# Six PSUM banks in a convolutional FFN, a later attention with two-part fp32r sums, and one sum moved to VectorE

## The chip, the cores and the metric

The kernel runs on one core of a Trainium2 chip. The metric is the device time of one execution in microseconds (us). Five engines work side by side, each through its own queue in program order: TensorE (PE: matmul, and PEld: its weight loads), VectorE (DVE), ScalarE (ACT), GpSimd (POOL) and SyncE (SP). PE multiplies a stationary operand (lhsT) by a moving one and writes to banks of PSUM; the other engines read the banks.

## The reference, cut to what matters

A sequence of 256 tokens of width 1024 passes through two blocks: a conformer convolution with a convolutional FFN, then two layers of FFN, mixer, FFN. The first layer's mixer is a recurrence, the second's is stick-breaking attention with 12 heads, together with an attention over 256 memory tokens. Three parts are touched here:

```python
def conv_ffn(h, w_up, dw_w, dw_b, w_down):
    u = causal_dwconv(h @ w_up, dw_w) + dw_b          # 3 taps
    gt, v = jnp.split(u, 2, axis=-1)
    return (jax.nn.silu(gt) * v) @ w_down

# stick-breaking attention, one block of 128 queries
z = einsum('bhtd,bhsd->bhts', q, k) * scale
log_keep = where(before, -softplus(z), 0.0)
later = cumsum(log_keep, axis=3, reverse=True) - log_keep
att = where(before, exp(log_sigmoid(z) + later), 0.0)
out = einsum('bhts,bhsd->bhtd', att, v)
```

The third is the mean and variance over the width after each mixer's output projection.

## The kernel before

Every large product is made of three fp32r products: activations and weights are each split into a high part and a low part. A weight unit (128 x 1024) is brought by DMA, cast to its high part by ACT (line 226, `whi`) and subtracted to its low part by DVE (line 235, `wlo`); `Stream.take` hands out units and issues the splits of units that come four later. The order on every engine is that of the program; there is no scheduler behind it.

**Convolutional FFN** (`ffn` with `conv`). For each of 22 hidden tiles j, PE makes two products into one PSUM bank (lines 372, 377 and 378, 48 matmuls), and `conv_gate` reads that bank: two ACT passes (line 885), four DVE passes (line 889), then silu (ACT, 894), a product (DVE, 895), a cast to `hx` high (ACT, 896) and a subtraction to `hx` low (DVE, 898). The bank is free again after line 889. Tiles 0 and 1 use banks acc2 and acc3, all later ones two `gu` banks in turn. Then the down projection (lines 372 and 384) runs for each of 8 outputs over all 22 `hx` tiles.

**Stick-breaking mixer** (`StickBreaking`). `weave` writes out one order of several tasks by a plan: each task yields its estimated PE time, DVE time and an extra delay; the plan keeps a clock for PE (`now`) and one for DVE, takes the first task in order of priority that is due, and where none is due it emits filler matmuls (`idle`, line 1455, 256 columns, one for each 0.11 us of the plan's gap). The main task makes the projections; attention has the highest priority; once the main task has ended, products of the output projection join. For each of 6 pairs of heads attention goes through these steps, shifted so that pair p's scores come before pair p-1's sums: `scores` (PE, then |z| and exp on ACT, lines 2298 and 2299), `log_keep` (Ln on ACT, line 2305, a DVE pass, line 2306, and a mask on POOL, line 2308), `attend` (three fp32 matmuls per head that add the running sums to the bank `z`, lines 2316, 2317 and 2319, a DVE pass and an exp on ACT), `values` (PE, lines 2332 and 2334, then a copy on ACT and a split, lines 625 and 626). The products of the output projection wait in the plan until five pairs have gone through `attend`. The constants for the mask and the sums (`sbc`, 320 KB) are brought by a DMA on ACT's queue at the start of the mixer.

**Output projection's end** (`gemm_tail`, at the end of three square products: line 1348 sums, line 1358 merge). The squares and values of tiles 0 to 3 are summed on POOL, those of tiles 4 and 6 on DVE, then the two sums are merged on DVE, tile 7 is taken out of its bank, and PE reduces the sums over partitions (line 1383).

Of the kernel before, what the change touches and what calls it, by code (L numbers as in the profile page):

```python
# [250 lines left out]
class Builder:  # L251
# [217 lines left out]
    def gemm_tail(self, acc, xs, st, on_tiles):  # L469


        def tile(w, b, o, i):
            c = slice((2 * i + o) * P, (2 * i + o) * P + P)
            self.mm3(acc[b][:, o, :], w[0][:, c], w[1][:, c], xs[i], False,
                     i == self.NT - 1)

        ws = [self.stream.take(False) for _ in range(2)]
        n = self.NT - 1
        for i0, i1 in ((0, n), (n, n + 1)):
            for b in range(2):  # L480
                for i in range(i0, i1):
                    for o in range(2):
                        tile(ws[b], b, o, i)
                if b == 0:
                    self.stream.split_hi()
        self.stream.split_hi()
        self.stream.split_lo()
        for b in range(2):
            on_tiles(2 * b, 2 * b + 2, acc[b])
            st.square(2 * b, 2 * b + 2)  # L490
            st.sum(2 * b, 2 * b + 2, "pool")
            if b == 0:
                self.stream.split_lo()
        ws = [self.stream.take(False) for _ in range(2)]
        self.stream.split_hi()
        for k in (4, 6, 5, 7):
            b, o = divmod(k, 2)
            for i in range(self.NT):
                tile(ws[b - 2], b, o, i)
            on_tiles(k, k + 1, acc[b][:, o:o + 1, :])  # L500
            st.square(k, k + 1)
            if k == 4:
                self.stream.split_lo()
            elif k == 5:
                st.sum(4, 5, "dve")
                st.sum(6, 7, "dve")
                st.sum(5, 6, None)
                st.merge()
        st.sum(7, 8, None)
        self.stream.split_lo()  # L510
# [270 lines left out]
    def ffn(self, conv, st, on_tile, li=None):  # L781


        self.mark("ffn")
        with self.pool("ffn") as self.fp:
            hs = [self.fp.tile([P, 2, T], F32R, name=f"hx{j}") for j in range(NF)]
            gates = []

            def gate(j, banks):
                make = self.conv_gate if conv else self.wide_gate  # L790
                gates.append(make(banks, j, hs[j][:, 0, :], hs[j][:, 1, :]))
                next(gates[-1])

            def advance():
                for g in list(gates):
                    if next(g, 0) == 0:
                        gates.remove(g)

            def banks(j):
                if conv:  # L800
                    return [self.acc_tile(2 + j) if j < 2 else self.gu_tile()]
                return [self.gu_tile() for _ in range(2)] if j % 3 == 0 else [
                    self.acc_tile(2 * (j % 3) - 2 + o) for o in range(2)]

            n = 0
            if self.pre is not None:
                for n in range(2):
                    gates.append(self.pre_gate(self.pre[2 * n:2 * n + 2], hs[n][:, 0, :], hs[n][:, 1, :]))
                    next(gates[-1])
                n = 2  # L810
                self.pre = None
            first = [banks(n), banks(n + 1)]
            (self.gemm_outs if conv else self.gemm_wides)(first[0] + first[1], self.xx)
            for j, bk in enumerate(first):
                gate(n + j, bk)
                advance()
                advance()
            for j in range(n + 2, NF):
                bk = banks(j)
                for o in range(2):  # L820
                    if conv:
                        self.gemm_out(bk[0][:, o, :], self.xx)
                    else:
                        self.gemm_wide(bk[o], self.xx)
                    advance()
                gate(j, bk)
            self.mark("down")
            self.preload(AF.Sqrt)
            if li is not None:
                self.raw_gains(li)  # L830
            i = 0
            for o in range(KD):
                acc = self.acc_tile(o % 4)
                for j in range(NF):
                    if i % 8 == 0:
                        wh, wl = self.stream.take()
                    c = slice(i % 8 * P, i % 8 * P + P)
                    self.mm_wide(acc, wh[:, c], wl[:, c], hs[j], j == 0, j == NF - 1)
                    i += 1
                    if o == 0 and j in (4, 8):  # L840
                        advance()
                on_tile(o, acc)
                st.square(o, o + 1)
                if li is not None:
                    self.raw_operand(o, li)
                st.sum(o, o + 1, "pool")
                if o < KD - 1:
                    self.pump(3.0)
# [1306 lines left out]
class StickBreaking(Mixer):  # L2155
# [25 lines left out]
    def project(self):  # L2181
        nc, b, mp = self.nc, self.b, self.mp
        sbc = mp.tile([P, 640], F32, name="sbc")
        nc.scalar.dma_start(out=sbc, in_=b.dr["consts_sb"])
        b.exp_and_log()
        self.sbk = {n: sbc[:, COFF[n][0]:sum(COFF[n])] for n, _ in CONSTS_SB}
        self.negones = mp.tile([P, P], F32, name="negones")
        nc.gpsimd.memset(self.negones, -1.0)
        ys = b.ys.rearrange("p k a t -> p (k a) t")
        self.V = ys[:, 0:6].rearrange("p (a f) t -> p a (f t)", a=2)  # L2190
        self.os = ys[:, 6:12]
        self.mq = ys[:, 14:16]
        self.qk, self.n_val = {}, 0
        pre, b.pre = b.pre, None
        for i in range(2):
            nc.scalar.copy(out=self.mq[:, i, :], in_=pre[2 + i])
        self.qk[0] = pre[:2]
        self.add(self.attention(), 1)
        for tl in range(2):
            self.add(self.mem_attention(tl, ys[:, 12 + tl]), SB_MEM)  # L2200
        early = [b.gu_tile() for _ in range(2)]
        yield from b.gemm_outs_parts(early, b.xx)
        for n in range(2):
            self.queries(n + 1, [early[n][:, i, :] for i in range(2)])
        self.mem_go = True
        for kind, i in SB_ORDER[2:]:
            if kind == "p":
                yield from self.pair(i)
                continue
            gu = b.gu_tile()  # L2210
            for u in range(2):
                list(b.gemm_tok(gu, b.xx, u))
                if u:
                    nc.scalar.copy(out=self.V[:, :, i * T:i * T + T], in_=gu)
                    self.n_val += 1
                yield 2.6, 1.1, 0.0
# [40 lines left out]

    def attention(self):

        yield 0.0, 0.0, 7.0  # L2260
        self.n_att = 0
        prev = None
        for p in range(NP + 1):
            cur = None
            if p < NP:
                wait = p not in self.qk
                while p not in self.qk:
                    yield
                if wait:
                    yield 0.0, 0.0, 1.0  # L2270
                cur = [self.scores(h, *self.qk[p]) for h in range(2)]
                yield 1.3, 0.9, 0.0
            if prev:
                for z, e in prev:
                    self.attend(z, e)
                self.n_att = p
                yield 1.7, 0.9, 0.0
            if cur:
                for z, e in cur:
                    self.log_keep(z, e)  # L2280
                yield 0.0, 0.9, 0.0
            if prev:
                while self.n_val <= (p - 1) // 2:
                    yield
                yield from self.values(p - 1, prev)
            prev = cur
# [21 lines left out]
        nc.gpsimd.tensor_tensor(out=d, in0=d,  # L2308
                                in1=self.sbk["tri"].unsqueeze(1).to_broadcast([P, 2, P]), op=ALU.mult)

    def attend(self, z, e):

        nc = self.nc
        mm = nc.tensor.matmul
        nt = self.sbk["negtri"]
        mm(z[:, 0:256], lhsT=nt, rhs=e[:, 0:256], start=False, stop=True, skip_group_check=True)  # L2316
        mm(z[:, 128:256], lhsT=self.negones, rhs=e[:, 256:384], start=False, stop=True,
           skip_group_check=True)
        mm(z[:, 256:384], lhsT=nt, rhs=e[:, 256:384], start=False, stop=True, skip_group_check=True)
        nc.vector.scalar_tensor_tensor(out=e, in0=z, scalar=0.0, in1=self.sbk["bias"], op0=ALU.min,  # L2320
                                       op1=ALU.add)
        nc.scalar.activation(out=e, in_=e, func=AF.Exp)
# [38 lines left out]
```

## Time and profile before

| | |
|---|---|
| median of 3 runs | 1480.18 us (1478.29 to 1483.04) |
| profiled execution, its own time | 1478.92 us |
| its span in the profile | 1477.1 us |
| busy: PE, DVE, ACT, POOL | 1412.8, 1074.2, 853.8, 120.2 us |
| mean granted TensorE clock | 0.976 of full |

The span runs from the first to the last instruction; the execution's own time is 1.8 us longer. Busy times are sums over an engine's instructions. Full clock is 2.4 GHz, the lower of the two levels is 1.2 GHz.

### The profile page before, as it was taken

The page shows a single profiled execution, that of the slowest core. Times are in us where ns is not written, and L with a number is a line of the kernel's source. Part 1 is how long each engine was busy: PE and PEld are TensorE (multiplying, and loading weights), DVE is VectorE, ACT ScalarE, POOL GpSimd, SP SyncE. Part 2 cuts the span into 40 slices and gives each one's busy share as a digit, 9 for nine tenths or more (in the row PEclk, how much of TensorE's full clock was granted, in tenths as well). Part 3 has the DMA queues.
Part 4 walks back from the last instruction along what each step waited for, and adds up shares of the span by engine and source line. Part 5 has one row for each costly group of instructions (what it writes and reads, how often), then busy time and mean ns, then how long its engine had stood idle before and what let it go on. Part 6 is the DMA issues. An engine that isn't in the chain of part 4 may idle for free. (4 is left out here: it accounts for less than half of the span.)

```text
span 1477.1 us, 26067 instructions
## 1 busy us (share of the span) xinstructions
PE 1412.8 (96%) x10664; PEld 1268.2 (86%) x10664; DVE 1074.2 (73%) x1698; ACT 853.8 (58%) x1509; POOL 120.2 (8%) x113
## 2 busy tenths in 40 slices
PE   8888899999999999998999999999999999999997
PEld 7868799998788888898798888888888888888886
DVE  8897788885777667897578776687766755787754
ACT  7686566685656535751346555466554666566542
POOL 1210100001000010040010000110001111100011
PEclk9998899999999999998999999999999999999998
DMA  9775445566355554330034555436545332265540
GB/s 377 295 232 191 178 145 198 200 222 218 124 201 191 200 187 149 109 121 3 2 114 171 200 179 192 184 133 226 195 176 199 126 141 86 95 225 194 198 174 29
DMA packets 39145, 250.38 MB, mean 170 GB/s; under 512 B 4337, under 2 KB 4849, under 8 KB 12274
## 3 DMA queue, kind: packets, MB, share of 16 engines
q1 hardware_dynamic: 38594, 247.60, 46.4%
q8 instruction: 84, 1.38, 0.4%
q10 hardware_dynamic: 432, 1.11, 0.2%
q14 instruction: 35, 0.29, 0.1%
HBM read 247.65 MB, written 1.05 MB: 168 GB/s over the span
## 5 line engine op out<-in xcount | busy, mean ns | idle before, releaser
L235 DVE TENSOR_TENSOR wlo<-wraw,whi 128x1024 fp32r<-128x1024 f32 x416 | 514.4, 1250 | 33.8 <-ACT whi L226 33.2
L226 ACT CAST whi<-wraw 128x1024 fp32r<-128x1024 f32 x416 | 426.4, 1045 | 23.8 <-PE acc L378 6.4
L384 PE MATMUL acc<-hx,whi 128*128 128x512 f32 x880 | 310.8, 398 | 0.0
L384 PE MATMUL acc<-xx,whi 128*128 128x512 f32 x816 | 284.1, 390 | 0.0
L372 PE MATMUL gu<-xx,wlo 128*128 128x256 f32 x1008 | 278.3, 281 | 2.8 <-ACT xx L625 1.7
L372 PE MATMUL acc<-xx,wlo 128*128 128x256 f32 x1008 | 279.4, 282 | 0.0
L372 PE MATMUL acc<-hx,wlo 128*128 128x256 f32 x880 | 247.5, 281 | 0.0
L384 PEld LDWEIGHTS acc<-hx,whi 128*128 128x128 f32 x880 | 165.4, 188 | 40.6
L372 PEld LDWEIGHTS gu<-xx,wlo 128*128 128x128 f32 x1008 | 188.6, 188 | 7.0 <-ACT xx L625 2.9
L372 PEld LDWEIGHTS acc<-xx,wlo 128*128 128x128 f32 x1008 | 189.6, 190 | 0.8
L384 PEld LDWEIGHTS acc<-xx,whi 128*128 128x128 f32 x816 | 153.2, 188 | 32.1
L372 PEld LDWEIGHTS acc<-hx,wlo 128*128 128x128 f32 x880 | 166.1, 189 | 0.0
L384 PE MATMUL gu<-xx,whi 128*128 128x512 f32 x432 | 150.9, 390 | 0.0
L377 PE MATMUL gu<-xx,whi 128*128 128x256 f32 x512 | 148.0, 289 | 2.3 <-ACT u L894 2.3
L378 PE MATMUL gu<-xx,whi 128*128 128x256 f32 x512 | 143.1, 279 | 0.0
L1331 ACT ACTIVATE ys<-ys 128x256 f32<-128x256 f32 (+1 forms) x66 | 28.6, 436 | 152.2 <-DVE ys L1249 135.2
L377 PEld LDWEIGHTS gu<-xx,whi 128*128 128x128 f32 x512 | 96.2, 188 | 9.2 <-issue 6.4
L378 PEld LDWEIGHTS gu<-xx,whi 128*128 128x128 f32 x512 | 96.3, 188 | 0.7 <-issue 0.7
L384 PEld LDWEIGHTS gu<-xx,whi 128*128 128x128 f32 x432 | 81.1, 188 | 17.0
L1348 POOL TENSOR_TENSOR nsum<-ys 128x512 f32<-128x512 f32 (+1 forms) x9 | 12.5, 1386 | 900.0 <-PE acc L384 451.8
L858 ACT COPY lows<-acc 128x256 f32<-128x256 f32 x55 | 20.6, 374 | 97.8 <-PE acc L384 97.7
L1247 DVE SCALAR_TENSOR_TENSOR ys<-xr,acc 128x256 f32<-128x256 f32 x32 | 13.5, 422 | 74.8 <-PE acc L384 74.8
(412 smaller groups left out, 2342.0 us busy)
## 6 DMA issues: line engine op xcount, KB each, us to landing
wraw<-in_w SPq DMA_DIRECT2D x208, 1024.0 KB, 4.8
mraw<-in_mod SPq DMA_DIRECT2D x48, 512.0 KB, 5.8
xr<-in_x SPq DMA_DIRECT2D x2, 512.0 KB, 4.3
m<-in_mem SPq DMA_DIRECT2D x1, 1024.0 KB, 8.2
out<-xr SPq DMA_DIRECT2D x3, 256.0 KB, 2.2
cst<-in_consts SPq DMA_DIRECT2D x1, 546.0 KB
lora<-in_lora ACTq DMA_DIRECT2D x1, 384.0 KB, 3.2
lora_g<-in_lora ACTq DMA_DIRECT2D x1, 384.0 KB, 3.8
```

The costliest lines, as they stand in the source:

```text
L226: b.nc.scalar.copy(out=hi, in_=raw)
L235: b.nc.vector.tensor_tensor(out=lo, in0=raw, in1=hi.bitcast(F32), op=ALU.subtract)
L372: self.nc.tensor.matmul(out, lhsT=wl, rhs=x[:, 0, :], start=start, stop=False, skip_group_check=True)
L377: mm(out, lhsT=wh, rhs=x[:, 0, :], start=start, stop=False, skip_group_check=True)
L378: mm(out, lhsT=wh, rhs=x[:, 1, :], start=False, stop=False, skip_group_check=True)
L384: self.nc.tensor.matmul(bank, lhsT=wh, rhs=x, start=False, stop=stop, skip_group_check=True)
L858: nc.scalar.copy(out=lows[:, 1, :], in_=banks[1][:, 1, :])
L1247: self.nc.vector.scalar_tensor_tensor(out=y, in0=self.xr[:, k, :], scalar=2 * ALPHA, in1=ps[:, 1, :], op0=ALU.mult, op1=ALU.add)
L1331: b.nc.scalar.activation(out=b.ys[:, k0:k1, 1, :], in_=y, func=AF.Square)
L1348: e.tensor_tensor(out=out[:, q:2, :], in0=prev[:, q:2, :], in1=t[:, q:2, :], op=ALU.add)
```

## The change

Two commits together. The convolutional FFN takes six banks in turn (acc2, acc3, gu, gu, acc0, acc1). In the stick-breaking mixer, attention may begin only once the early query products are copied out (`self.early`) instead of 7 us into the plan; the softplus values are split by ACT and DVE into two fp32r parts (`e_parts`, a step of its own with 1.1 us of DVE in the plan), and each running sum is made of two fp32r matmuls instead of one fp32; the constant operands are made in fp32r by two ACT passes that read `sbc`, where POOL set one of them before. In `gemm_tail` the sum over tile 3 goes from POOL to DVE.

```diff
@@ gemm_tail
             st.square(2 * b, 2 * b + 2)
-            st.sum(2 * b, 2 * b + 2, "pool")
+            st.sum(2 * b, 2 * b + 2 - b, "pool")
             if b == 0:
                 self.stream.split_lo()
+            else:
+                st.sum(3, 4, "dve")
@@ ffn, banks
                 if conv:
-                    return [self.acc_tile(2 + j) if j < 2 else self.gu_tile()]
+                    i = (2, 3, None, None, 0, 1)[j % 6]
+                    return [self.gu_tile() if i is None else self.acc_tile(i)]
@@ StickBreaking.project
-        self.negones = mp.tile([P, P], F32, name="negones")
-        nc.gpsimd.memset(self.negones, -1.0)
+        self.negs = mp.tile([P, 2, P], F32R, name="negs")
+        nc.scalar.copy(out=self.negs[:, 0, :], in_=self.sbk["negtri"])
+        nc.scalar.activation(out=self.negs[:, 1, :], in_=self.sbk["negtri"], func=AF.Copy, scale=0.0,
+                             bias=-1.0)
...
-        self.qk, self.n_val = {}, 0
+        self.qk, self.n_val, self.early = {}, 0, False
...
-        self.mem_go = True
+        self.mem_go = self.early = True
@@ attention
-        yield 0.0, 0.0, 7.0
         self.n_att = 0
+        while not self.early:
+            yield
...
             if prev:
-                for z, e in prev:
-                    self.attend(z, e)
+                parts = [self.e_parts(e) for _, e in prev]
+                yield 0.0, 1.1, 0.0
+                for (z, e), x in zip(prev, parts):
+                    self.attend(z, e, x)
                 self.n_att = p
-                yield 1.7, 0.9, 0.0
+                yield 0.9, 0.9, 0.0
@@ attend
+    def e_parts(self, e):
+        x = self.mp.tile([P, 2, 384], F32R, name="ep", bufs=2)
+        self.b.split_act(x[:, 0, :], x[:, 1, :], e)
+        return x
...
-        nt = self.sbk["negtri"]
-        mm(z[:, 0:256], lhsT=nt, rhs=e[:, 0:256], start=False, stop=True, skip_group_check=True)
-        mm(z[:, 128:256], lhsT=self.negones, rhs=e[:, 256:384], start=False, stop=True,
-           skip_group_check=True)
-        mm(z[:, 256:384], lhsT=nt, rhs=e[:, 256:384], start=False, stop=True, skip_group_check=True)
+        for i, (w, out, c) in enumerate(((0, z[:, 0:256], slice(0, 256)), (1, z[:, 128:256], slice(256, 384)),
+                                         (0, z[:, 256:384], slice(256, 384)))):
+            for q in range(2):
+                mm(out, lhsT=self.negs[:, w, :], rhs=x[:, q, c], start=False, stop=True,
+                   skip_group_check=True)
```

The order of instructions moves with it. On ACT, at the start of the mixer, these rows stand behind the DMA of the constants before (`pre` are the first pair's products, `q` and `k` the early queries' copies, lines 2231 and 2232):

```order
L2184 DMA sbc<-in_consts_sb 128x640
L342 ACT_TABLE_LOAD
L2196 COPY ys<-pre_8478 128x256
L2196 COPY ys<-pre_8479 128x256
L226 CAST whi<-wraw 128x1024 x2
L2298 ACTIVATE e<-z 128x384
L2299 ACTIVATE e<-e 128x384
L2298 ACTIVATE e<-z 128x384
L2299 ACTIVATE e<-e 128x384
L2231 ACTIVATE q<-gu 128x256
L2232 COPY k<-gu 128x256
```

And these of the change (its lines 2192 and 2193 make the fp32r constants, 2237 and 2238 are the copies):

```order
L2187 DMA sbc<-in_consts_sb 128x640
L342 ACT_TABLE_LOAD
L2192 CAST negs<-sbc 128x128
L2193 ACTIVATE negs<-sbc 128x128
L2202 COPY ys<-pre_8478 128x256
L2202 COPY ys<-pre_8479 128x256
L226 CAST whi<-wraw 128x1024 x2
L2237 ACTIVATE q<-gu 128x256
L2238 COPY k<-gu 128x256
```

The first pair's four passes moved from ahead of the copies to behind them, and two passes that read the DMA's data came in ahead of everything.

On PE, behind the main task's last product, these rows stand before, from the first filler (line 1455) to the fifth pair's sums, which the output projection's products follow:

```order
L1455 MATMUL gu<-whi 128x256 x3
L2294 MATMUL z<-q,k 128x256
L2295 MATMUL z<-q,k 128x128
L2294 MATMUL z<-q,k 128x256
L2295 MATMUL z<-q,k 128x128
L1455 MATMUL gu<-whi 128x256 x2
L1535 MATMUL gu<-mpt_13032,memv 64x256
L1535 MATMUL gu<-mpt_13033,memv 64x256
L2316 MATMUL z<-e,sbc 128x256
L2317 MATMUL z<-e,negones 128x128
```

And of the change, at the same place, the last one and a half of three such rounds (fillers are its line 1458, sums 2332, values 2346 and 2348, scores 2303 and 2304):

```order
L1458 MATMUL gu<-whi 128x256 x22
L2332 MATMUL z<-ep,negs 128x256 x2
L2332 MATMUL z<-ep,negs 128x128 x4
L2332 MATMUL z<-ep,negs 128x256 x2
L2332 MATMUL z<-ep,negs 128x128 x4
L1458 MATMUL gu<-whi 128x256 x20
L2346 MATMUL gu<-e,ys 64x256
L2348 MATMUL gu<-e,ys 64x128
L2346 MATMUL gu<-e,ys 64x256
L2348 MATMUL gu<-e,ys 64x128
L1458 MATMUL gu<-whi 128x256 x11
L2303 MATMUL z<-q,k 128x256
```

Before, four pairs had gone through `attend` when the main task ended and 5 fillers followed; of the change two have, a third follows at once, and then come fillers of 17, 11, 22, 20, 11 and 22 matmuls, 103 in all, with the rest of the third to fifth pairs between them.

On DVE, at the end of the attention's output projection, these rows stand before:

```order
L1235 SCALAR_TENSOR_TENSOR ys<-xr,acc 128x256 x2
L1348 TENSOR_TENSOR nsum<-ys 128x512
L1358 TENSOR_TENSOR nsum<-nsum 128x512
L1235 SCALAR_TENSOR_TENSOR ys<-xr,acc 128x256
L235 TENSOR_TENSOR wlo<-wraw,whi 128x1024
```

And of the change:

```order
L1238 SCALAR_TENSOR_TENSOR ys<-xr,acc 128x256 x2
L1351 TENSOR_TENSOR nsum<-ys 128x512
L1351 TENSOR_TENSOR nsum<-nsum,ys 128x512
L1361 TENSOR_TENSOR nsum<-nsum 128x512
L1238 SCALAR_TENSOR_TENSOR ys<-xr,acc 128x256
```

DVE has one sum more ahead of the merge, and POOL's queue one sum fewer.

## Rows read from the trace of the kernel before

**Rows 1.** Page, part 1: busy us, share of the span, instructions.

```profile
PE 1412.8 (96%) x10664; PEld 1268.2 (86%) x10664; DVE 1074.2 (73%) x1698; ACT 853.8 (58%) x1509; POOL 120.2 (8%) x113
```

**Rows 2.** Windows of the mixer: length; busy PE, PEld, DVE, ACT, POOL; clock, DMA.

```profile
1178.00:1182.20 4.20, 4.20 (x24) 4.20 (x24) 2.86 (x4) 4.20 (x8) 0.00 (x0) 0.60 0.65 218
1182.20:1238.00 55.80, 55.80 (x414) 48.63 (x415) 31.33 (x53) 37.19 (x84) 9.22 (x10) 1.00 0.31 112
```

**Rows 3.** Timeline, convolutional FFN, PE: start, us, [idle before <-releaser].

```profile
206.48 0.35 PE L377 MATMUL gu<-xx,whi 128*128 128x256 f32 x1 [2.28 <-ACT u L894]
...
307.47 0.40 PE L384 MATMUL acc<-hx,whi 128*128 128x512 f32 x1
...
314.83 0.43 PE L384 MATMUL acc<-hx,whi 128*128 128x512 f32 x1
```

**Rows 4.** Timeline, start of the mixer, ACT and PE.

```profile
1170.39 0.33 ACTq L2184 DMA_DIRECT2D sbc<-in_consts_sb  x1
...
1171.14 0.71 PE L2294 MATMUL z<-pre,pre 64*128 64x256 f32 x4
...
1172.00 0.74 PE L423 MATMUL gu<-xx,whi 128*128 128x256 f32 x4
...
1172.80 0.71 ACT L2196 COPY ys<-pre 128x256 f32<-128x256 f32 x2
...
1173.42 2.00 ACT L226 CAST whi<-wraw 128x1024 fp32r<-128x1024 f32 x2
...
1177.45 0.36 ACT L2232 COPY k<-gu 128x256 f32<-128x256 f32 x1
...
1177.87 0.39 PE L448 MATMUL gu<-whi,xx 128*128 128x256 f32 x1 [2.80 <-ACT k L2232]
```

**Rows 5.** Timeline, PE: sums over partitions, one column each.

```profile
1272.20 1.05 PE L1383 MATMUL st<-inv,nsum 128*128 128x1 f32 x8 [0.81 <-DVE nsum L1358]
1273.12 1.03 PE L1383 MATMUL st<-inv,ys 128*128 128x1 f32 x8
```

**Rows 6.** Timeline, convolutional FFN, ACT and DVE.

```profile
203.64 1.01 ACT L885 ACTIVATE u<-gu,vecs 128x256 f32<-128x256 f32 x2
...
307.56 1.02 ACT L885 ACTIVATE u<-gu,vecs 128x256 f32<-128x256 f32 x2
...
314.28 0.42 DVE L898 TENSOR_TENSOR hx<-u,hx 128x256 fp32r<-128x256 f32 x1
```

**Rows 7.** Timeline, DVE: sums and a merge behind two of the square products.

```profile
765.08 0.68 DVE L1348 TENSOR_TENSOR nsum<-ys 128x512 f32<-128x512 f32 x1
766.93 0.69 DVE L1358 TENSOR_TENSOR nsum<-nsum 128x512 f32<-128x512 f32 x1 [1.16 <-POOL nsum L1348]
...
1269.56 1.79 DVE L1348 TENSOR_TENSOR nsum<-ys 128x512 f32<-128x512 f32 x1
```

**Rows 8.** DMA issues, start of the mixer: KB each, median us to landing.

```profile
sbc<-in_consts_sb ACTq DMA_DIRECT2D x1, 320.0 KB, 2.8
```

**Rows 9.** Timeline, ACT: first and last of the four passes behind a pair's scores.

```profile
1240.40 0.49 ACT L2298 ACTIVATE e<-z 128x384 f32<-128x384 f32 x1 [0.25 <-PE z L2295]
...
1241.85 0.52 ACT L2299 ACTIVATE e<-e 128x384 f32<-128x384 f32 x1
```

**Rows 10.** Timeline, PE: start of one pair's sums, and the product behind them.

```profile
1230.18 0.59 PE L2316 MATMUL z<-e,sbc 128*128 128x256 f32 x2
...
1231.86 0.36 PE L448 MATMUL gu<-whi,xx 128*128 128x256 f32 x1
```

**Rows 11.** Timeline, PE: two products of the output projection, six matmuls apart.

```profile
1269.61 0.28 PE L372 MATMUL acc<-ox,wlo 128*128 128x256 f32 x1
...
1270.32 0.28 PE L372 MATMUL acc<-ox,wlo 128*128 128x256 f32 x1
```

**Rows 12.** Weight loads by line: busy us, mean ns.

```profile
L378 PEld LDWEIGHTS acc<-ox,whi 128*128 128x128 f32 x64 | 12.1, 188 | 0.0
...
L2317 PEld LDWEIGHTS z<-e,negones 128*128 128x128 f32 x24 | 4.6, 190 | 0.6
```

More of the change, by code (lines that the diff above doesn't have):

```diff
@@ L2309, in log_keep, with attend @@
                                 in1=self.sbk["tri"].unsqueeze(1).to_broadcast([P, 2, P]), op=ALU.mult)
-    def attend(self, z, e):
+    def e_parts(self, e):
+        x = self.mp.tile([P, 2, 384], F32R, name="ep", bufs=2)
+        self.b.split_act(x[:, 0, :], x[:, 1, :], e)
+        return x
+    def attend(self, z, e, x):
         nc = self.nc
         mm = nc.tensor.matmul
-        nt = self.sbk["negtri"]
-        mm(z[:, 0:256], lhsT=nt, rhs=e[:, 0:256], start=False, stop=True, skip_group_check=True)
-        mm(z[:, 128:256], lhsT=self.negones, rhs=e[:, 256:384], start=False, stop=True,
-           skip_group_check=True)
-        mm(z[:, 256:384], lhsT=nt, rhs=e[:, 256:384], start=False, stop=True, skip_group_check=True)
+        for i, (w, out, c) in enumerate(((0, z[:, 0:256], slice(0, 256)), (1, z[:, 128:256], slice(256, 384)),
[3 more added lines that the diff above has]
+                   skip_group_check=True)
         nc.vector.scalar_tensor_tensor(out=e, in0=z, scalar=0.0, in1=self.sbk["bias"], op0=ALU.min,
```

## The prediction, made before the changed kernel ran

> **What bounds the kernel now.** I read the page's busy shares first: PE is busy for 96% of the span, DVE for 73%, ACT for 58% [rows 1]. So work that PE loses or gains counts fully, and the other engines count only where PE waits for them. The windows of the attention mixer come next, since most of the change is there: from 1182.2 to 1238 us PE is busy without a gap and at full clock, while DVE and ACT are a little over half busy [rows 2]. Then I looked for PE's waits at the places that the change touches. There are three kinds: 2.28 us in the convolutional FFN at 206.48 [rows 3], 2.80 us at the start of the mixer at 1177.87 [rows 4], and short ones where a square product's sums are reduced, as the 0.81 us at 1272.20 [rows 5].
>
> **Six banks: nothing, since the wait moves.** With two banks PE must wait at tile 4 until the gate of tile 2 has read its bank; with six it runs on, and gets about 2.4 us ahead (the 2.28 us and the restart). But the gates of ACT and DVE do not run faster for it. Their first pass starts at 203.64 for tile 2 and at 307.56 for tile 21, which is 20 starts and 19 periods of 5.47 us [rows 6], against 5.6 us a tile on PE (18 tiles from 206.48 to the first wide matmul of the down projection at 307.47 [rows 3]). Before the change PE never makes ACT or DVE wait in there: their waits are for each other. The last link of this chain is the low part of tile 21, from 314.28 to 314.70 [rows 6]. PE's wide matmul of tile 21 starts at 314.83 (307.47 and 21 steps of 0.35) and takes 0.43, where that of tile 0 took 0.40 [rows 3]: it arrives just as its operand does. What PE gains at 206 it must therefore wait for at about 312.4, in the down projection's first output. I take 0; the other bound is a gain of 2.4.
>
> **Sum over tile 3 on DVE: -0.9.** Behind the recurrence's projection DVE ends its sum at 765.76 and then waits 1.16 us for POOL [rows 7]. Of the change POOL has one sum fewer and is done by then, and DVE has one more of 0.68: the merge starts at about 766.5 in place of 766.93, 0.4 earlier. Behind the attention's projection DVE's sum takes 1.79 us beside a POOL sum, where the other took 0.68, and ends at 1271.35 [rows 7]; two sums of 0.68 with no POOL sum beside them end at 1271.0, 0.4 earlier. In the first of the three square products a sum has half as many elements, and I take 0.1. Each merge is on the chain to the next norm. Bounds: 0 (POOL's remaining sums run late too) and -1.4.
>
> **Mixer, start: about 0.** ACT's queue gets two passes that need the constants. Their DMA is issued at 1170.39 [rows 4] and lands 2.8 us later [rows 8], at 1173.2; ACT was ready for its next copies at 1172.80 [rows 4]. Two passes of 128 columns (0.28 each, less than the 0.36 a piece of the 256-column copies [rows 4]) end at 1173.75, so copies and casts run 0.95 late. The first pair's four passes, about 1.9 us from the end of the casts on [rows 9], no longer stand ahead of the query copies. The first `k` comes at 1177.0 in place of 1177.81 (1177.45 + 0.36), and PE restarts at 1177.06: -0.8. But the first pair's scores, 0.86 us of PE from 1171.14 to 1172.00 [rows 4], were covered by this wait and now come behind it: +0.86. After the wait, PE's clock stood at 0.60 for 4.2 us, mostly at the lower level [rows 2]; I assume the same again, and 1.7 us less is the other bound.
>
> **The sums in fp32r: -2.0.** Before, a pair's six fp32 matmuls take 1231.86 - 1230.18 = 1.68 us, or 0.84 to 0.87 a head with the step to the next form [rows 10]. Now a head has two fp32r matmuls of 256 columns and four of 128. The 256-column form takes 0.118 (six steps from 1269.61 to 1270.32 [rows 11]). No fp32r matmul of 128 columns is in the trace. The nearest rows: one-column matmuls, each with its own load of 128 x 128 weights, come every 0.115 us (8 from 1272.20 to 1273.12) [rows 5], and an fp32r load takes as long as an fp32 one, 188 and 190 ns [rows 12]. So the load sets the pace. With 0.115 a head takes 0.24 + 0.46 = 0.70, and 12 heads save 12 x 0.165 = 2.0. Bounds: 0.06 a matmul (half of the 256-column form), which saves another 2.6, and 0.22 (0.84 less the 256-column matmul's share, the half of it, over two), which turns the saving into a loss of 3. The Trainium skill (TensorE: Matmul & The Clock Gate, Back-to-back issue gap) gives about 81 ns a matmul for a stream of loads and matmuls of 128 columns; by that the saving would be 3.6. The one-column rows here are slower than that figure, and the sum goes by the rows.
>
> **Fillers in the mixer's tail: +11.5.** This is the term that decides. The order shows 103 filler matmuls where 5 stood: attention starts later in the plan, each pair has a step more, and the main task runs out with four pairs still to be summed in place of two, so that nothing is left to put between their steps. PE takes them in order, whether they are needed or not. A matmul of that shape takes 0.118 [rows 11]: 98 x 0.118 = 11.5. Bounds: 10.5 (0.107 each) and 12. Nothing hides it, since PE had no gap in this stretch.
>
> **Waits that the fillers do not cover: +0.8.** In a tail round 22 fillers (2.6 us) stand between a pair's scores and the sums of the pair before. In that time ACT makes the scores' four passes, 0.1 behind them and 1.97 long (1240.40 to 1242.37 [rows 9]), then casts the other pair's first part and DVE subtracts it, each about as long as one of these passes (0.5): 3.1 us against 2.6. The high part's matmul can go first, so about 0.4 is left, in two rounds. Bounds 0 and 2.
>
> **Sum.** 0 - 0.9 - 0.8 + 0.9 - 2.0 + 11.5 + 0.8 = +9.5 us. From the profiled execution's own 1478.92 that gives 1488.4; the median of the runs shown is 1.26 above that execution, which gives 1489.7. I predict 1489, 0.6% slower.
>
> **The rivals.**
> *The short matmuls take 0.22 each.* For it: they have as many columns as the fp32 ones that take this. Against it: one pass over the columns in place of two. A head then takes 1.12, which adds 5.0 to the sum, less the 0.8 of waits that it covers: about 1493.
> *They are cheaper than the loads suggest*, 0.06: 2.6 less, 1486.4. It needs loads that hide behind matmuls half as long, and the one-column rows speak against that.
> *Six banks keep their gain.* If the gates speed up once their banks are apart, PE keeps the 2.4: 1486.6. Against it: the 5.47 us period, in which no wait for PE stands.
> *The fillers cost little* (the other side). A filler repeats one operand and one weight tile; if such a matmul passed in 0.067 us or less, 98 of them would cost under 6.5 and the time would be within 4.4 us of before, and at 0.02 there would be no change. Against it: it is a 256-column fp32r matmul with a load of its own, like the products that take 0.118.
>
> **How the numbers follow.** About 0.3%, 4.4 us, is what a measurement of this kernel tells from no change. Chances: forecast 0.62, slow short matmuls 0.12, cheap ones 0.10, the banks' gain kept 0.07, fillers cheap or several terms low together 0.09. The forecast alone reaches from 1486.5 to 1492 (clock 1.7, sums 0.9, fillers 1, waits 1, the spread of the runs). The range goes up to 1494 for the first rival and down to 1484.8, which takes in the second and the third. Slower by over 0.3% comes to 0.88, within it to 0.10, faster to 0.02.
>
> **What would show it.** In the FFN, no wait at 206, and waits of 2.4 us in all at tile 21 of the down projection's first output, released by DVE's or ACT's `hx`; if they are missing, the bank step is wrong. At the mixer's start, ACT waiting for the constants' DMA and PE restarting near 1177. In the sums, a spacing near 0.115 for the 128-column matmuls. In the tail, 103 fillers of 0.118 and waits under 0.5 ahead of two pairs' sums; at the merges, DVE free of waits for POOL. The prediction fails if PE waits inside the main task's stretch, where I count none, or if the fillers' time comes out below 7 us.

## The result, and the profile after

The changed kernel took 1487.19 us (median of 5 runs, 1485.57 to 1489.32) against 1480.07 us of the kernel before, measured beside it (5 runs, 1478.08 to 1483.04): 1.0051 times as long, 95% interval 1.004 to 1.0063. The forecast was 1489, 0.6% slower. The profiled execution took 1485.57 us (its span is 1483.8), 6.65 more than the one of before. At 120 us, ahead of everything that the change touches, it is 1.4 us ahead of that one, so what it loses behind this point is 8.0 us. For this reason stretches are compared below, not times from the start of the span.

Page, part 1, of the change (engine, busy us, share of the span, instructions):

```profile
PE 1424.7 (96%) x10762; PEld 1281.8 (86%) x10762; DVE 1078.6 (73%) x1713; ACT 859.5 (58%) x1523; POOL 116.6 (8%) x109
```

PE is 11.9 us busier than in [rows 1] and has as large a share of the span. A busy share does not say that the work is of use.

Windows of the mixer of the change (columns as in [rows 2]):

```profile
1174.50:1178.00 3.50, 3.47 (x28) 3.32 (x30) 2.88 (x3) 3.37 (x5) 0.00 (x0) 1.00 0.72 253
1178.00:1182.20 4.20, 4.20 (x35) 3.85 (x32) 1.50 (x2) 3.50 (x7) 0.00 (x0) 1.00 0.99 375
1182.20:1228.90 46.70, 46.62 (x354) 41.01 (x353) 27.22 (x49) 33.20 (x76) 6.22 (x6) 1.00 0.29 106
1229.30:1250.40 21.10, 20.82 (x166) 18.55 (x165) 7.74 (x16) 11.83 (x28) 2.83 (x4) 1.00 0.14 50
```

The clock is full right after the restart, where [rows 2] has 0.60. The last window is the loss: PE is busy for 20.8 of 21.1 us, while ACT is busy for 11.8 and DVE for 7.7. Its rows (timeline of the change, PE; 1458 are fillers, 2332 sums):

```profile
1229.31 2.60 PE L1458 MATMUL gu<-whi 128*128 128x256 f32 x17
...
1233.50 1.58 PE L1458 MATMUL gu<-whi 128*128 128x256 f32 x11
1235.01 0.71 PE L2303 MATMUL z<-q,k 64*128 64x256 f32 x4
...
1238.60 1.86 PE L2332 MATMUL z<-ep,negs 128*128 128x256 f32 x12
1240.30 2.60 PE L1458 MATMUL gu<-whi 128*128 128x256 f32 x20
...
1246.00 2.89 PE L1458 MATMUL gu<-whi 128*128 128x256 f32 x22
1248.73 1.86 PE L2332 MATMUL z<-ep,negs 128*128 128x256 f32 x12
1250.43 0.33 PE L377 MATMUL acc<-ox,whi 128*128 128x256 f32 x1
```

Before, the main task's last product and the first product of the output projection stood at these times (timeline of before, PE):

```profile
1237.49 0.27 PE L452 MATMUL gu<-whi,xx 128*128 128x256 f32 x1
...
1243.52 0.37 PE L377 MATMUL acc<-ox,whi 128*128 128x256 f32 x1
```

That is 6.0 us; now the second comes 22.9 us behind the first (1250.43 against 1227.50). From PE's restart to that product it is 75.90 us (1174.53 to 1250.43), before 65.65 (1177.87 to 1243.52): +10.25, more than the whole loss.

Start of the mixer in the change (timeline, ACT and PE, as [rows 4]):

```profile
1170.93 0.30 ACT L2192 CAST negs<-sbc 128x128 fp32r<-128x128 f32 x1 [0.45 <-DMA sbc<-in_consts_sb]
...
1174.12 0.36 ACT L2238 COPY k<-gu 128x256 f32<-128x256 f32 x1
...
1174.53 0.39 PE L448 MATMUL gu<-whi,xx 128*128 128x256 f32 x1 [2.01 <-ACT k L2238]
```

The convolutional FFN of the change (timeline, PE and ACT, as [rows 3] and [rows 6]):

```profile
304.39 0.39 PE L384 MATMUL acc<-hx,whi 128*128 128x512 f32 x1
...
306.93 1.28 ACT L338 ACT_TABLE_LOAD   x1
...
309.39 1.28 ACT L897 ACT_TABLE_LOAD   x1
310.68 0.42 ACT L897 ACTIVATE u<-u 128x256 f32<-128x256 f32 x1
...
311.41 0.39 PE L384 MATMUL acc<-hx,whi 128*128 128x512 f32 x1
...
311.59 0.40 ACT L899 CAST hx<-u 128x256 fp32r<-128x256 f32 x1 [0.49 <-DVE u L898]
...
312.05 0.38 PE L372 MATMUL acc<-hx,wlo 128*128 128x256 f32 x1 [0.25 <-ACT hx L899]
...
313.08 0.50 PE L384 MATMUL acc<-hx,whi 128*128 128x512 f32 x1 [0.65 <-DVE hx L901]
```

No wait is left at 206 us; instead PE waits at tile 21, twice, for `hx`. Two table loads stand ahead of that tile's silu on ACT, one for the square root that is needed later (line 338) and one that fetches silu's table back. The merge behind the attention's projection (timeline of the change, PE, as [rows 5]):

```profile
1276.68 0.95 PE L1386 MATMUL st<-inv,ys 128*128 128x1 f32 x8
1278.13 1.05 PE L1386 MATMUL st<-inv,nsum 128*128 128x1 f32 x8 [0.50 <-DVE nsum L1361]
```

### The profile page after: what moved, and what is told of

Same layout as the page of the kernel before. It is cut to its first block, busy times and chain, and to the rows that moved or that the text cites. A ratio compares the mean times of both kernels' runs of the same rounds, so it can differ in the third digit from the quotient of the medians.

```text
span 1483.8 us, 26273 instructions
## 1 busy us (share of the span) xinstructions
PE 1424.7 (96%) x10762; PEld 1281.8 (86%) x10762; DVE 1078.6 (73%) x1713; ACT 859.5 (58%) x1523; POOL 116.6 (8%) x109
## 5 line engine op out<-in xcount | busy, mean ns | idle before, releaser
L372 PE MATMUL acc<-xx,wlo 128*128 128x256 f32 x1200 | 333.5, 282 | 0.0
L372 PE MATMUL gu<-xx,wlo 128*128 128x256 f32 x816 | 225.6, 283 | 1.6 <-ACT xx L627 0.8
L372 PEld LDWEIGHTS acc<-xx,wlo 128*128 128x128 f32 x1200 | 226.1, 190 | 0.8
L372 PEld LDWEIGHTS gu<-xx,wlo 128*128 128x128 f32 x816 | 153.7, 190 | 5.1 <-ACT xx L688 1.9
L384 PEld LDWEIGHTS gu<-xx,whi 128*128 128x128 f32 x432 | 81.1, 188 | 17.0
L377 PE MATMUL gu<-xx,whi 128*128 128x256 f32 x320 | 94.5, 295 | 0.0
L377 PE MATMUL acc<-xx,whi 128*128 128x256 f32 x320 | 91.1, 285 | 1.9 <-DVE ys L1182 1.1
L378 PE MATMUL acc<-xx,whi 128*128 128x256 f32 x320 | 90.9, 284 | 0.3 <-DVE xx L2141 0.3
L378 PE MATMUL gu<-xx,whi 128*128 128x256 f32 x320 | 90.1, 282 | 0.0
L1250 DVE SCALAR_TENSOR_TENSOR ys<-xr,acc 128x256 f32<-128x256 f32 x32 | 13.5, 422 | 75.1 <-PE acc L384 75.1
```

The source lines that it names most:

```text
L372: self.nc.tensor.matmul(out, lhsT=wl, rhs=x[:, 0, :], start=start, stop=False, skip_group_check=True)
L377: mm(out, lhsT=wh, rhs=x[:, 0, :], start=start, stop=False, skip_group_check=True)
L378: mm(out, lhsT=wh, rhs=x[:, 1, :], start=False, stop=False, skip_group_check=True)
L384: self.nc.tensor.matmul(bank, lhsT=wh, rhs=x, start=False, stop=stop, skip_group_check=True)
L1250: self.nc.vector.scalar_tensor_tensor(out=y, in0=self.xr[:, k, :], scalar=2 * ALPHA, in1=ps[:, 1, :], op0=ALU.mult, op1=ALU.add)
```

## Experiments

Every ratio is to the kernel before, measured beside the run, and the range behind it is its 95% interval. "The mixer" is the stretch from PE's restart behind the wait for `k` to the first product of the output projection: 65.65 us before, 75.90 with the change. "The FFN" is the stretch from its tile 2 to the sums over partitions that follow its last output: 176.43 and 176.28 us.

**The change's parts, each alone on the kernel before.** Six banks (`banks_alone`):

```diff
-                    return [self.acc_tile(2 + j) if j < 2 else self.gu_tile()]
+                    i = (2, 3, None, None, 0, 1)[j % 6]
+                    return [self.gu_tile() if i is None else self.acc_tile(i)]
```

> The kernel before with the six banks alone. Theory (the gates of ACT and DVE set the end of this stage): PE's wait of 2.28 us at the fifth tile goes, and waits for the last tile's hx of together about 2 us come in the down projection's first output; the low part of the last tile ends at the same distance from the first gate's pass; time within 0.3 us of before, which the comparison calls the same. Rival (the banks' gain is kept): 2.4 us less, a ratio of 0.9984, and no such wait.

1.0007 (0.9995 to 1.0018). The wait moved as in the change (0.29 and 0.65 us at tile 21, none at 206), the FFN took 176.30 us. The move is shown; a gain over 0.05% is excluded.

The sum on VectorE (`sum_alone`):

```diff
-            st.sum(2 * b, 2 * b + 2, "pool")
+            st.sum(2 * b, 2 * b + 2 - b, "pool")
...
+            else:
+                st.sum(3, 4, "dve")
```

> The kernel before with the sum over tile 3 moved to DVE, alone. Theory, from the trace of the change: about 0.3 to 0.5 us less behind the recurrence's projection, nothing behind the first square product and 0 to 0.3 behind the attention's; in all 0.3 to 0.8 us less, a ratio near 0.9996. Rival (as the prediction had it): 0.9 less, with 0.4 behind each of the two later products.

0.9997 (0.9985 to 1.001). The traces show what the time can't: behind the recurrence's projection the way from the projection's end to the merged sums' reduction is 0.26 us shorter.

The later start (`late_alone`):

```diff
-        yield 0.0, 0.0, 7.0
         self.n_att = 0
+        while not self.early:
+            yield
```

> The kernel before with attention begun only once the early queries are copied out, sums still in fp32. Its order has 25 fillers in the mixer's tail where before has 5. Theory (fillers are what the change costs, and the added step of the plan makes most of them): fillers +2.5 us, scores of the first pair uncovered +0.9, PE restarts about 1.7 earlier at the mixer's start, and if the clock does not fall after that shorter wait another 1.5 less: between -0.5 and +1.5 us. Rival (the late start is what costs): +7 us or more, as in the whole change.

1.0006 (0.9997 to 1.0016), with 25 fillers, as the theory had it. The fp32r sums, their parts and the plan's step, with the early start of before (`fp32r_alone`; an excerpt, the rest of the edit is that of the change):

```diff
+                parts = [self.e_parts(e) for _, e in prev]
+                yield 0.0, 1.1, 0.0
+                for (z, e), x in zip(prev, parts):
+                    self.attend(z, e, x)
```

> The kernel before with the softplus in two fp32r parts and its added step in the plan, attention started as before. Its order has 78 fillers in the mixer's tail. Theory (the added step of the plan costs): fillers +9, sums 2.6 less, waits for the parts in two rounds +0.8, the constants' DMA holds ACT at the mixer's start +0.9: about +8 us, a ratio near 1.0055. Rival (late start costs, the fp32r sums pay): 2 to 3 us less than before.

1.0067 (1.0054 to 1.008), with 78 fillers. The loss belongs to this part.

**The plan's step without the work it stands for** (`step_alone`). One line in the kernel before, whose sums stay fp32:

```diff
             if prev:
+                yield 0.0, 1.1, 0.0
                 for z, e in prev:
```

> The kernel before (fp32 sums, no parts, early start, no six banks, no sum on VectorE) with one line more: the plan's step of 1.1 us ahead of a pair's sums, for work that this kernel does not have. By its order TensorE then has 78 fillers instead of 5. Theory (the loss is the estimate in the plan, which spends the projection's steps two pairs early and fills the rest): 73 fillers at 0.12 us, 9 us slower than before, 1487 to 1489. Rival (fillers only stand where the parts make TensorE wait; without parts they shift waits that are there): within 3 us of before, 1477 to 1482.

1486.87 us, 1.0061 (1.0047 to 1.0075), 0.13 us under the theory's range. The mixer's two ends (timeline of this run, PE):

```profile
1175.16 0.38 PE L448 MATMUL gu<-whi,xx 128*128 128x256 f32 x1 [2.75 <-ACT k L2232]
...
1249.22 0.37 PE L377 MATMUL acc<-ox,whi 128*128 128x256 f32 x1
```

It took 74.06 us, 8.4 more than before, for 73 fillers more, with the clock behind its first wait as low as before (0.63 and 0.62 over 4.5 us). This one estimate in the plan costs as much as the whole change.

**Twice as many fillers, and none.** Both on the change, by a method of the attention's own. Twice as many:

```diff
+    def idle(self, us):
+        super().idle(2 * us)
```

> The change, with twice as many fillers in each of the six places (206 instead of 103). Theory (each filler takes about 0.12 us of a busy TensorE and nothing hides it): 12 to 13 us slower than the change, about 1496 to 1500. Rival (fillers lie in waits): less than 4 us slower.

1498.87 us, 1.0138 (1.0123 to 1.0153), 12.9 us more than the change's share (0.87% of 1479). Each of the 103 added fillers cost 0.125 us. None:

```diff
+    def idle(self, us):
+        pass
```

> The change, with the fillers (single matmuls whose results nobody reads) left out of the attention phase; what is computed is the same. Theory (TensorE carries 103 fillers that cover no wait of the tail, about 12.6 us more than the kernel before had): the rounds after the projection's own steps ran out shrink by up to those 13.5 us, but ScalarE and VectorE then need about 7.2 us a round instead of 9.4, so 4 to 6 us come back (span 1478 to 1480) with waits of TensorE of 1 to 2 us a round in the fillers' places; if the granted clock falls in those waits, 2 to 3 us of it are lost. Rival (fillers only fill waits that are there anyway): within 1 us of the change, 1483 to 1485.

1486.26 us, 1.0048 (1.0035 to 1.006): nothing came back, and the rival was right on the time. Timeline (PE) and windows of the run without fillers:

```profile
1238.14 0.38 PE L2335 MATMUL z<-ep,negs 128*128 128x256 f32 x1 [2.46 <-ACT ep L627]
1238.73 2.61 PE L2335 MATMUL z<-ep,negs 128*128 128x256 f32 x11 [0.21 <-DVE ep L628]
...
1248.01 0.39 PE L2335 MATMUL z<-ep,negs 128*128 128x256 f32 x1 [2.46 <-ACT ep L627]
```

```profile
1229.30:1238.10 8.80, 4.88 (x26) 2.98 (x25) 3.07 (x7) 6.03 (x16) 1.40 (x2) 0.81 0.35 119
1238.10:1251.00 12.90, 9.97 (x40) 7.81 (x41) 5.17 (x10) 6.21 (x14) 1.41 (x2) 0.64 0.00 0
```

Half of the fillers' 13.5 us turned into waits (1.49, 2.46, 0.21, 2.46 and 0.21 us: 6.8 in all); the rest, by difference, went into matmuls at a lower clock (0.64 to 0.81 against 1.00 in the change's window). So the fillers are where the time shows, but not what causes it: that is a tail in which PE has nothing else to do while a pair's chain runs.

**No step in the plan, early start** (`early_no_step`). The change, with PE's order in the mixer as before (5 fillers):

```diff
+        yield 0.0, 0.0, 7.0
         self.n_att = 0
-        while not self.early:
-            yield
...
-                yield 0.0, 1.1, 0.0
+                yield 0.0, 0.0, 0.0
```

> The change, with the attention started at once as in the kernel before, and the step of 1.1 us of ScalarE's and VectorE's work that the plan was given for the two parts set to nothing: 5 fillers instead of 103. Theory (the loss is the fillers, which the plan's own estimate calls up): the 12 us of fillers go; the pairs' sums stay 0.4 us shorter each, and TensorE waits for the parts of e about 1 us a pair where no other step stands between; in sum 1477 to 1483, thus 4 to 10 us faster than the change. Rival (the parts themselves make the rounds longer, ScalarE and VectorE bind the attention): 1485 to 1489, as the change, with the fillers' time now as waits.

1498.05 us, 1.0128 (1.0114 to 1.0141), about 11 us slower than the change where 4 to 10 faster was expected. Both the theory and the rival fell: without the step the kernel is worse still. The mixer took 84.02 us. Timeline of this run around the third pair's sums, POOL, ACT and PE:

```profile
1216.05 1.49 POOL L2316 TENSOR_TENSOR e<-e,sbc 128x256 f32<-128x256 f32 x2 [16.50 <-DVE e L2314]
...
1221.25 0.49 ACT L2306 ACTIVATE e<-z 128x384 f32<-128x384 f32 x1 [0.60 <-PE z L2303]
...
1222.71 0.53 ACT L2307 ACTIVATE e<-e 128x384 f32<-128x384 f32 x1
1223.14 0.36 ACT L2237 ACTIVATE q<-gu 128x256 f32<-128x256 f32 x1
1223.40 0.36 ACT L2238 COPY k<-gu 128x256 f32<-128x256 f32 x1
1223.66 0.66 ACT L1533 COPY mpt<-r 128x256 f32<-128x256 f32 x2
1224.18 1.08 ACT L226 CAST whi<-wraw 128x1024 fp32r<-128x1024 f32 x1
1225.13 0.95 ACT L627 CAST ep<-e 128x384 fp32r<-128x384 f32 x2
...
1225.72 2.56 PE L2331 MATMUL z<-ep,negs 128*128 128x256 f32 x9 [2.44 <-ACT ep L627]
```

`e` is complete when POOL ends its mask, at 1217.54. The cast of `ep` starts 7.6 us later: in the code it stands behind the next pair's scores, so on ACT behind their four passes and all that has been queued since. Five pairs' sums in the mixer waited 9.7 us in all, and behind the waits the clock fell: of the four windows from 1182 to 1253 us (cut at 1200, 1220 and 1240) three have 0.81 to 0.87, one 1.00. That gave a new theory: the parts are late by their place in ACT's queue, not by their cost.

**The parts made a round earlier.** As the run before, with one move:

```diff
             if prev:
-                parts = [self.e_parts(e) for _, e in prev]
-                yield 0.0, 0.0, 0.0
...
                 yield from self.values(p - 1, prev)
+            if cur:
+                parts = [self.e_parts(e) for _, e in cur]
             prev = cur
```

> The change with the attention started at once, no step for the parts in the plan (TensorE's order is that of the run early_no_step, 5 fillers), and the two parts of e made a place earlier: at the end of the round that made e, ahead of the next pair's scores on ScalarE, not behind them. Theory (the parts are late because their casts stand on ScalarE behind the next pair's four passes over its scores, 2.0 us, though e is finished before those): the waits of 1.1 to 2.4 us for ep go, and with them the clock falls; the pairs' sums stay 0.4 us shorter; 1474 to 1482, 16 to 24 us less than early_no_step. Against it: at the first pair the casts wait for GpSimd ahead of the copies of q and k, which can lengthen the wait for k by up to 2.4 us. Rival (ScalarE's and VectorE's added work of 0.9 and 1.0 us a pair binds wherever it stands): 1490 to 1498, as early_no_step.

1478.71 us, 0.9999 (0.999 to 1.0007), 19 us less than the run before, at the same order on PE. Timeline of this run, POOL, ACT and PE, at the same pair:

```profile
1210.69 1.49 POOL L2316 TENSOR_TENSOR e<-e,sbc 128x256 f32<-128x256 f32 x2 [12.76 <-DVE e L2314]
...
1215.18 0.93 ACT L627 CAST ep<-e 128x384 fp32r<-128x384 f32 x2
...
1216.00 0.50 ACT L2306 ACTIVATE e<-z 128x384 f32<-128x384 f32 x1
...
1217.76 1.47 PE L2331 MATMUL z<-ep,negs 128*128 128x256 f32 x12
```

The casts now run while PE still works on other things, and the sums start without a wait. The mixer took 63.74 us, 1.9 less than before: the shorter sums of five pairs come through. The theory held. The loss that it named at the start did not come: the wait for `k` was 3.67 us, against 3.64 in the run before, where the casts stood late. Behind the mixer the sixth pair's sums still waited for their parts, 1.2 us in all:

```profile
1248.38 0.38 PE L2331 MATMUL z<-ep,negs 128*128 128x256 f32 x1 [0.52 <-ACT ep L627]
...
1249.42 1.46 PE L2331 MATMUL z<-ep,negs 128*128 128x256 f32 x11 [0.66 <-DVE ep L628]
```

**The table load moved.** On the change, the load for the square root goes behind the last gate:

```diff
-            self.preload(AF.Sqrt)
+            if not conv:
+                self.preload(AF.Sqrt)
...
                     if o == 0 and j in (4, 8):
                         advance()
+                        if conv and j == 8:
+                            self.preload(AF.Sqrt)
```

> The change, with ScalarE's load of the square-root table in the convolutional FFN (two table loads of 1.28 us just ahead of the last gate step of token tile 21) put behind the last gate. Theory (with six banks the wait of 2.3 us did not go: it stands at tile 21 of the down projection, because ScalarE loads two tables before that tile's gate): the waits of 0.25 and 0.65 us near 312 us go, and the stretch from the FFN's start to its last output is about 1 us shorter than in the change (175 instead of 176.3 us); the time 1 us less or not to be told apart. Rival (tile 21 is late by the gate chain of 5.46 us a tile itself): no change in that stretch.

1484.63 us, 1.0035 (1.0023 to 1.0047); the interval overlaps with the change's, but the FFN shows it: 174.76 us, 1.5 less than in the change, and none of the eleven profiles without this move is under 176.28. One wait is left (timeline, PE, of this run):

```profile
311.84 0.32 PE L372 MATMUL acc<-hx,wlo 128*128 128x256 f32 x1
312.80 0.51 PE L384 MATMUL acc<-hx,whi 128*128 128x512 f32 x1 [0.65 <-DVE hx L904]
```

So tile 21 was late by the two loads and, for the 0.65 that is left, by its gate. The theory had said that this wait would go too.

**Two versions made of what held.** The change with the parts ahead (late start, no step in the plan, 25 fillers) and the moved load:

```diff
-                parts = [self.e_parts(e) for _, e in prev]
-                yield 0.0, 1.1, 0.0
...
+            if cur:
+                parts = [self.e_parts(e) for _, e in cur]
...
+                        if conv and j == 8:
+                            self.preload(AF.Sqrt)
```

> The change (attention started late, as in it) with the parts made ahead of the next pair's scores, no step for them in the plan (25 fillers, TensorE's order in the attention that of late_alone), and the square-root table loaded behind the last gate of the convolutional FFN. Theory: the attention as in late_alone less 0.4 us at each of six pairs, the FFN 1.5 us shorter than in the change; 1474 to 1479, at or under the kernel before. Rival (the parts bind wherever they stand): 1484 to 1490.

1475.26 us, 0.9987 (0.9974 to 0.9999). And the kernel before with six banks, the sum on VectorE and the moved load, its attention as it was:

```diff
+                    i = (2, 3, None, None, 0, 1)[j % 6]
...
+                st.sum(3, 4, "dve")
...
+                        if conv and j == 8:
+                            self.preload(AF.Sqrt)
```

> The kernel before with the six banks, one sum on VectorE and the square-root table loaded behind the last gate of the convolutional FFN; its attention unchanged (early, fp32 sums). Theory (with six banks, the wait of 2.3 us in the FFN ends only once tile 21's gate is no longer behind two table loads): 1.5 us in the FFN and 0.3 to 0.5 us in the two square products; 1475.5 to 1478, 1 to 3 us under the kernel before. Rival (the wait moves once more, to the gate chain of the tile before): no change, 1478 to 1480.

1475.04 us, 0.9979 (0.9967 to 0.9991), the FFN 174.84 us. Both are under both kernels, the first by an interval that barely excludes no difference, and neither is told from the other. Not run: the moved load without six banks, and the parts ahead with the early start and the moved load together.

## Why the prediction was right

The time lies in the range, the sign and the deciding term held. Term by term, in the profiled executions:

**Six banks, 0.** Right in size, and the wait went where it was said to go: the FFN is 0.15 us shorter. The reason was half right. I put the end of tile 21 down to the gates' period alone and did not read the two table loads of 1.28 us ahead of its silu; once the load is moved, 1.5 us are gained with six banks. The waits in the change come to 1.3 us (two matmuls 0.4 and 0.9 late), not 2.4. In the run without fillers PE came to this tile 1.06 us earlier, and there they are 2.4 (1.5 and 0.9; timeline of that run, PE):

```profile
310.35 0.39 PE L384 MATMUL acc<-hx,whi 128*128 128x512 f32 x1
312.05 0.38 PE L372 MATMUL acc<-hx,wlo 128*128 128x256 f32 x1 [1.31 <-ACT hx L899]
```

**The sum on DVE, -0.9.** Over-sized: -0.25 behind the recurrence, -0.31 behind the attention, 0.0 at the first. I let the sums follow each other at their duration of 0.68; in the change they start 0.79 apart. The reading of the 1.79 us was not shown either: I put it down to a POOL sum beside it, but the sum of 0.68 had one beside it too. It had started 0.06 us ahead of POOL's, the one of 1.79 started 0.04 behind (timeline of before, POOL, beside [rows 7]):

```profile
765.14 1.75 POOL L1348 TENSOR_TENSOR nsum<-nsum,ys 128x512 f32<-128x512 f32 x1
...
1269.52 1.28 POOL L1348 TENSOR_TENSOR nsum<-nsum,ys 128x512 f32<-128x512 f32 x1
```

In all five profiles with the sum on POOL the one behind the attention took 1.79 to 1.81; in the change, with no POOL sum beside it, it took 0.68. At the attention's end 0.46 was lost again, since the 16 one-column matmuls took 2.27 us in place of 1.81 at a granted clock of 0.80.

**The mixer's start, +0.06.** The restart came 1.04 us sooner (forecast 0.8), and the first pair's scores cost their 0.86. The assumption that failed is the clock behind the wait: it stayed full, and the first 24 matmuls took 3.03 us in place of 4.55. That is as much as the whole sum was off (+9.5 against the 8.0 that this execution lost behind 120 us), but that is partly luck: the other misses, up to 1.1 us each, cancel in part, with 1.1 more for the fillers and 0.3 less gained by the sum on DVE, against 0.3 more gained by the fp32r sums and 0.2 by the restart. The clock itself was not luck. In all six profiles whose wait here was 1.16 to 2.10 us it stayed full; in seven of the eight with 2.75 to 3.69 us it fell, to 0.62 or 0.63 over the next 4.5 us.

**The sums, -2.0.** A pair takes 1.30 us in place of 1.68, six times 0.38: -2.3. With the 256-column matmul at 0.118, a 128-column one took 0.104 (1.30 less 4 x 0.118, over 8), near the 0.115 of the one-column rows. The 0.104 are 28% above the Trainium skill's figure for such a stream (TensorE: Matmul & The Clock Gate, Back-to-back issue gap: about 81 ns); the rows decide.

**The fillers, +11.5.** The six blocks take 2.53, 1.51, 2.73, 2.53, 1.50 and 2.73 us to the next form, 13.5 against 0.96 before: +12.6. 103 at 0.118 are 12.2; the rest is the steps between forms at six blocks, which the forecast left out, and about 0.4 in the first block, most of it a gap behind the seventh filler; what PE waited for there is not shown.

**The waits, +0.8.** Two tail pairs took 1.70 where the others took 1.30 to 1.32: +0.78.

The terms inside the mixer add up to 10.8 (12.6 + 0.86 + 0.78 - 1.9 - 1.5), the stretch has 10.25; 0.5 is not attributed.

So the accounting was right, but it stopped one question early. I called the fillers the term that decides and wrote that nothing hides them. For added ones that holds (0.125 us each), but not for those that stand there, which gave nothing back when they were left out; that run shows that they stood for waits that the change itself had made, and the two runs without the plan's step (1.0128 and 0.9999, same order on PE) show where these came from: ACT's casts of the parts stand behind the next pair's passes. The step of 1.1 us in the plan covered for that place, and paid with the main task's products, which ran out two pairs early. That the plan's step by itself makes the loss, and that it can be left out once the casts stand earlier, are both shown.

## What to carry to other kernels

Where a new piece of work makes a consumer wait, look first at its place in its engine's queue and when its input was complete: here the move of two casts by one round was worth 19 us in the version without the plan's step, and with it the kernel took as long as the one that has no casts (0.9999). In an order written by a plan, an added estimate is paid for by the work that fills gaps later: count what is left of it at the end. Taking filler matmuls away says little about what causes the time that they fill: here the wait and the clock behind it took their place.

## What was not expected of the hardware

Behind waits of PE of about the same length the clock is not the same from execution to execution. Before, the granted clock was 0.60 behind 2.80 us at the mixer's start [rows 2, 4], and full behind the 2.28 us at 206 us. With the change it was full behind 2.01 us. At 206 us, in the five profiles with two banks, it stayed full behind 2.28 us twice and fell behind 2.27, 2.38 and 2.39. In the run without fillers it fell at tile 21 of the FFN; windows of that run, ahead of and behind PE's restart:

```profile
303.40:310.00 6.60, 6.60 (x40) 5.79 (x40) 5.46 (x9) 5.31 (x8) 0.00 (x0) 1.00 0.61 231
...
312.50:316.50 4.00, 3.42 (x11) 2.95 (x12) 4.00 (x6) 2.79 (x5) 0.00 (x0) 0.61 0.65 231
```

The FFN then took 177.81 us, 1.5 more than in the change. The same two lengths stand in the kernels with two banks (176.43 in the kernel before, 177.97 in the run of the sum alone), so a single profile compares such a stretch to no better than 1.5 us. With the moved load, in three kernels, it was 174.76 to 174.84. At tile 21 with six banks the clock goes with the wait: behind 0.25 and 0.29 us, and then 0.65, it stayed full (176.28 and 176.30 us); behind 1.30 to 1.32, and then 0.65, it fell in four profiles (177.79 to 177.83). The longer wait comes from a faster PE ahead of it: in each 20 us from 210 to 290 us PE started 172 matmuls in the change and 174 in the run without fillers, both at a granted clock of 1.00. Why PE's pace differs there, and why about 2.3 us at 206 us ends one way or the other, is open.
